# Seven block products for eight in the gate and up projections of a decoder trunk, with three chunks of inner units and the residual kept in y

## The chip, the core and the metric

The kernel runs on one core of a Trainium2 chip. The metric is device time in microseconds (us) of one execution, as the median of several. Engines are named as in the profile: PE (TensorE matmuls), PEld (its weight loads), DVE (VectorE), ACT (ScalarE), POOL (GpSimd), SP (SyncE, which here only issues DMAs).

## What is computed

A trunk of two layers over 528 tokens (16 meta tokens and 512 of the sequence), width 1024. Each layer has a feed-forward block (FFN), a mixer (a convolution branch and a recurrent branch), and a second FFN, each followed by a layer norm over the scaled input plus the block's output. The part that matters here:

```python
D_MODEL = 1024; SEQ = 512; DEPTH = 2; N_META = 16; D_FF = 2816
LN_EPS = 1e-5; ALPHA = (2 * DEPTH) ** 0.25

def _swiglu(x, wg, wu, wd):
    return (jax.nn.silu(x @ wg) * (x @ wu)) @ wd

for l in range(DEPTH):
    h = _layer_norm(ALPHA * h + 0.5 * _swiglu(h, ffn1_wg[l], ffn1_wu[l], ffn1_wd[l]), ln1_g[l], ln1_b[l])
    m = _mixer(h, ...)
    h = _layer_norm(ALPHA * h + m, ln2_g[l], ln2_b[l])
    h = _layer_norm(ALPHA * h + 0.5 * _swiglu(h, ffn2_wg[l], ffn2_wu[l], ffn2_wd[l]), ln3_g[l], ln3_b[l])
return h[:, N_META:]
```

All of it is float32. `wg` and `wu` are 1024 x 2816, `wd` is 2816 x 1024.

## The kernel before

**Data and precision.** Activations lie transposed, features on the 128 partitions and tokens along the free side: x is 8 k-tiles of 128 features by 528 tokens. Every float32 operand of a large product is split into two float32r parts, `hi` (a cast on ACT) and `lo` (the remainder, a subtraction on DVE; `split`, L101). A product of two split operands is three matmuls per k-tile: hi by hi, hi by lo, lo by hi (`mac1`, L190). The lo by lo part is left out.

**Weights.** `wunit` (L106) brings one block of up to 8 k-tiles by 128 columns (512 KB) from HBM into a `w_raw` tile (two buffers) by a DMA on SP's queue, casts it to `w_hi` on ACT (L128) and forms `w_lo` on DVE (L139). With `dma=True`, which only 32 of the mixer's blocks use, ACT writes the negated `hi` part into `w_lo` (L132) and an accumulating DMA issued by POOL adds `w_raw` to it (L133). The `w_hi`, `w_lo` pairs come from a ring of pools (`self.wring`), eight pairs in an FFN's body.

**An FFN** (`ffn`, L425). Its tokens are handled in two halves of 264 (256 in the last FFN, which leaves out the meta tokens); `tok[h]` is one half. The 2816 inner units are 22 tiles of 128, handled in two chunks of 11. In a chunk:

- `up(fc, f)`: load one gate and one up block (8 k-tiles each), and for each half multiply both with x into two PSUM banks (48 matmuls), then silu on ACT (L453), the product on DVE (L454), and the split into `hh`, `hl` (L103, L104).
- `down(fh, o)`: for one of 8 tiles of outputs, multiply `hh`, `hl` of the 11 units with two blocks of `wd`, for each half into one bank. The first chunk's result goes into `y` scaled by 0.5 (ACT, L474), and `residual` adds ALPHA times both parts of x (DVE, L420). The second chunk adds to `y` (L477) and to the running sum `ssum` (L415) of the norm.

`stream` (L151) takes the jobs in this order: load, then half 0 and half 1. The last three down jobs (`TAIL`) are run half by half: all three for half 0, then all three for half 1, so that the norm of half 0 (`layer_norm`, L364; mean and variance by matmuls with a matrix of ones, L371 and L390; square root and reciprocal, L391 and L392; then 8 tiles of x's two parts, L396, L406, L407) runs beside the products of half 1. The weights of the next stage are fetched in between (`fetch_ahead`). The first products of the next stage on half 0 (`heads(0)`, or the mixer's first three blocks) run beside the norm of half 1.

**Order.** A scheduler at build time fixes the order of each engine's instructions from the program's order, priorities and its own estimates. At run time each engine takes its instructions in that order and waits for what they need. Buffers are reused under the same waits.

PSUM has eight banks: six for products (`mm`) and two for the norms (`st`). The constants `smask` and `e1`, which only the mixer uses, lie in the constant pool.

Of the kernel before, what the change touches and what calls it, by code (L numbers as in the profile page):

```python
# [24 lines left out]
FT = F // P  # L25
FH = FT // 2
TAPS = 31
# [62 lines left out]
class Trunk:  # L90
# [10 lines left out]
    def split(self, x, hi, lo):  # L101

        return (self.nc.scalar.copy(hi, x),  # L103
                self.nc.vector.tensor_tensor(lo, x, hi.bitcast(F32), op=ALU.subtract))  # L104

    def wunit(self, *srcs, dst=None, dma=False):  # L106

        srcs = [s if isinstance(s, tuple) else (slice(0, P), s) for s in srcs]
        kt = srcs[0][1].shape[1]
        raw = self.wp.tile([P, KT, P], F32, name="w_raw", bufs=WB[0])  # L110
        if dst is None:
            pool, bufs = self.wring[self.wi % len(self.wring)]
            self.wi += 1
            dst = [pool.tile([P, KT, P], F32R, name=x, bufs=bufs) for x in ("w_hi", "w_lo")]
        hi, lo = dst
        for r, src in srcs:
            load = self.nc.sync.dma_start(out=raw[r, :kt], in_=src)
            if self.behind is not None:
                self.nosync(load, self.behind)
                self.behind = None  # L120
        n = kt // self.cuts
        for i in range(0, kt, n):
            k = slice(i, i + n)
            if self.cuts == 1 or not CUTA:
                continue
            self.nc.scalar.copy(hi[:, k], raw[:, k])
        if self.cuts == 1 or not CUTA:
            copy = self.nc.scalar.copy(hi[:, :kt], raw[:, :kt])  # L128
            if self.first is not None:
                self.nosync(copy, self.first[0])  # L130
        if dma:
            self.nc.scalar.activation(lo[:, :kt], raw[:, :kt], AF.Copy, scale=-1.0)  # L132
            self.nc.gpsimd.dma_start(out=lo[:, :kt].bitcast(F32), in_=raw[:, :kt], accum_op=ALU.add)  # L133
            return hi, lo
        if not CUTD:
            n = kt
        for i in range(0, kt, n):
            k = slice(i, i + n)
            sub = self.nc.vector.tensor_tensor(lo[:, k], raw[:, k], hi[:, k].bitcast(F32),  # L139
                                               op=ALU.subtract)  # L140
# [48 lines left out]

    def mac1(self, pm, w, x, s, nk, xk=0, first=True, last=True):  # L190

        hi, lo = w
        xh, xl = x
        for k in range(nk):
            for j, (a, b) in enumerate(((hi, xh), (hi, xl), (lo, xh))):
                self.nc.tensor.matmul(pm, a[:, k, :], b[:, xk + k, s],  # L196
                                      start=first and k == 0 and j == 0,
                                      stop=last and k == nk - 1 and j == 2)
            yield
# [23 lines left out]
    def setup(self):  # L223
# [29 lines left out]
        for h in range(2):  # L253
            for i in range(4):
# [3 lines left out]
                                        channel_multiplier=1)  # L258
        self.smask = cp.tile([P, T], F32, name="smask")
        nc.vector.memset(self.smask, 1.0)  # L260
        nc.vector.memset(self.smask[:, 0:1], 0.0)
        nc.vector.memset(self.smask[:, NM::C], 0.0)
        self.eps = cp.tile([P, 1], F32, name="eps")
        nc.vector.memset(self.eps, LN_EPS)
        self.e1 = [cp.tile([P, T + 1], F32, name=f"e1_{i}") for i in range(2)]
        for e in self.e1:
            nc.vector.memset(e[:, 0:1], 0.0)
        self.e1i = 0
        self.xh = cp.tile([P, KT, T], F32R, name="xh")
# [93 lines left out]

    def layer_norm(self, h, y, ssum, t0, n, gname, bname, pool, st, dst, vec, silu=False):  # L364

# [7 lines left out]
        for g in range(2):  # L373
# [5 lines left out]
            sqs.append(sq)  # L379
        rstd = pool.tile([P, 264], F32, name="ln_rstd", bufs=2)  # L380
        if SQ:

            nc.scalar.activation(rstd[:, 0:1], self.eps, AF.Sqrt)
        for sq in sqs:
# [26 lines left out]
    def add_sum(self, ssum, y, o, s):  # L411
        if o == 1:
            return self.nc.vector.tensor_tensor(ssum[:, s], y[:, 0, s], y[:, 1, s], op=ALU.add)
        elif o > 1:
            return self.nc.vector.tensor_tensor(ssum[:, s], ssum[:, s], y[:, o, s], op=ALU.add)  # L415

    def residual(self, y, o, s):

        for part in self.x:
            self.nc.vector.scalar_tensor_tensor(  # L420
                y[:, o, s], part[:, o, s].bitcast(F32), ALPHA, y[:, o, s],
                op0=ALU.mult, op1=ALU.add)


    def ffn(self, l, which, t0, n, gname, bname, pre, final=False, head=None, extra=()):  # L425
# [15 lines left out]
        def up(fc, f):  # L441
# [9 lines left out]
            def evac(h, ps):  # L451
                g = fp.tile([P, 264], F32, name="g", bufs=3)[:, :n]
                nc.scalar.activation(g, ps[0][:, :n], AF.Silu)  # L453
# [4 lines left out]

        def down(fh, o):
            cs = slice(o * P, (o + 1) * P)  # L460
            cuts = (0, 6), (6, FH)

            def load():
                return [self.wunit(wd[:, fh * FH + a:fh * FH + b, cs]) for a, b in cuts]

            def mac(w, h):
                pd = mm()
                return pd, [self.mac1(pd[:, :n], wi, (hh, hl), tok[h], b - a, a, a == 0, b == FH)
                            for wi, (a, b) in zip(w, cuts)]

            def evac(h, pd):
                yv = y[:, o, tok[h]]
                if fh == 0:
                    nc.scalar.mul(yv, pd[:, :n], 0.5)  # L474
                    self.residual(y, o, tok[h])
                else:
                    nc.vector.scalar_tensor_tensor(yv, pd[:, :n], 0.5, yv,  # L477
                                                   op0=ALU.mult, op1=ALU.add)
# [12 lines left out]
        def room():  # L491
# [3 lines left out]
            ssum = fp.tile([P, T], F32, name="ssum")  # L495
            hh, hl = (fp.tile([P, FH, T], F32R, name=x) for x in ("hh", "hl"))
            return y, ssum, lambda: fp.tile([P, 4, 264], F32, name="ln_sq", bufs=2).rearrange(
# [76 lines left out]
    def store(self, y, t0, n, pool, mm):  # L574
        nc = self.nc
        for i in range(SEQ // P):
            a = t0 + i * P
            ot = pool.tile([P, D], F32, name="ot", bufs=2)
            for g in range(2):
# [8 lines left out]
    def mixer(self, l, last, pre, more):  # L588
# [26 lines left out]
        self.ring(self.w0)  # L615
        mpool, self.mp = self.enter(f"mix{l}")
        self.places()
        cpool, self.cvp = self.enter(f"conv{l}")
# [915 lines left out]
```

## Time and profile before

| | |
|---|---|
| three runs | 3175.49, 3195.22 and 3193.57 us, median 3193.57 us |
| the profiled execution | span 3187.1 us from its first to its last instruction; its own time with what lies around the span is not given beside it |
| PE | 3086.5 us busy, 97%, 27172 matmuls |
| DVE | 1870.3 us, 59% |
| ACT | 1227.7 us, 39% |
| POOL | 52.4 us, 2% |
| DMA | 343.25 MB, mean 108 GB/s; queue of SP 34.1% of the 16 engines' span, queue of POOL 3.3% |
| mean granted TensorE clock | 0.976 |

In the lists of groups, a row is line, engine, operation, output <- inputs, shapes and count, then busy us, mean ns of one, then the engine's idle time just before these instructions and what ended it. A row of the windows gives a stretch (us from the span's start), its length, then the busy us and counts on PE, PEld, DVE, ACT and POOL, the granted clock (1.00 is full speed), the DMA engines' busy share and the GB/s moved. Matmuls overlap in the pipeline: the mean of one is longer than the distance from one to the next. Timeline rows are start, duration, engine, line, what; in square brackets the idle time before and what ended it.

### The profile page before, as it was taken

What the parts mean: (1) busy time and instruction counts of PE and PEld (TensorE: products, weight loads), DVE (VectorE), ACT (ScalarE), POOL (GpSimd) and SP (SyncE); (2) the same over time, 40 slices, a digit from 0 to 9 for tenths busy, and PEclk for the clock granted to TensorE, in tenths of its full rate; (3) what the DMA queues carried; (4) which work ended last, traced back from release to release, by engine and by line L of the source; (5) the groups of instructions that cost most, each with busy time, mean ns of one, the idle gap of its engine ahead of it and who ended that gap; (6) DMA issues with size and microseconds to landing.
All of it is one profiled execution on the core that took longest, in us unless ns stands there. A gap on an engine that the chain in (4) does not pass through costs nothing.

```text
span 3187.1 us, 64710 instructions
## 1 busy us (share of the span) xinstructions
PE 3086.5 (97%) x27172; PEld 2956.2 (93%) x27172; DVE 1870.3 (59%) x3811; ACT 1227.7 (39%) x2223; POOL 52.4 (2%) x132
## 2 busy tenths in 40 slices
PE   9999999999999899999999999999999999999998
PEld 8999989888888899999989999898888889999997
DVE  4343377888775766343363433778887758653435
ACT  4232154344454544232142321543454445242322
POOL 0000000000000000000000000000000000000000
PEclk9999999999998899999999999999998999999998
DMA  5232234334354552232232322343353555332321
GB/s 151 73 108 84 82 121 152 94 94 121 102 138 119 168 153 79 74 107 85 82 93 73 107 85 82 115 154 99 97 132 92 141 135 177 112 108 82 111 73 54
DMA packets 576434, 343.25 MB, mean 108 GB/s; under 512 B 87501, under 2 KB 539457, under 8 KB 576143
## 3 DMA queue, kind: packets, MB, share of 16 engines
q1 hardware_dynamic: 565422, 308.49, 34.1%
q0 software_dynamic: 6112, 22.10, 3.3%
q10 hardware_dynamic: 4608, 8.52, 0.7%
q8 instruction: 213, 3.49, 0.5%
q14 instruction: 79, 0.64, 0.1%
HBM read 270.81 MB, written 47.12 MB: 100 GB/s over the span
## 4 chain that ended last, share of the span: by engine, by line
PE 83%; DVE 6%; ACT 4%; DMA 4%; issue 2%; SPq 1%; ACTq 0%; DVEq 0%; POOLq 0%
PE mm L196 53%; PE mm L214 16%; PE sc L1127 2%; PE sc L1046 1%; PE ch L1221 1%; PE tr L1196 1%; DVE w_lo L139 1%; PE tr L1204 1%; PE ch L1213 1%; PE sc L799 1%; SPq L1095 1%; DMA a<-ascr 1%; ACT w_hi L128 1%; PE sc L931 1%; PE tr L1191 1%
## 5 line engine op out<-in xcount | busy, mean ns | idle before, releaser
L196 PE MATMUL mm<-xh,w_hi 128*128 128x264 f32 (+1 forms) x2880 | 818.6, 285 | 17.4 <-ACT xh L406 16.0
L196 PE MATMUL mm<-xh,w_lo 128*128 128x264 f32 (+1 forms) x2880 | 819.8, 285 | 0.5 <-DVE w_lo L139 0.5
L196 PE MATMUL mm<-xl,w_hi 128*128 128x264 f32 (+1 forms) x2880 | 818.1, 284 | 0.3 <-DVE xl L407 0.2
L139 DVE TENSOR_TENSOR w_lo<-w_raw,w_hi 128x1024 fp32r<-128x1024 f32 (+2 forms) x456 | 485.1, 1064 | 432.7 <-ACT w_hi L128 420.1
L128 ACT CAST w_hi<-w_raw 128x1024 fp32r<-128x1024 f32 (+2 forms) x400 | 385.3, 964 | 763.4 <-PE mm L196 524.6
L196 PEld LDWEIGHTS mm<-xh,w_hi 128*128 128x128 f32 x2880 | 544.7, 190 | 21.1 <-ACT xh L406 18.2
L196 PEld LDWEIGHTS mm<-xh,w_lo 128*128 128x128 f32 x2880 | 546.2, 190 | 0.8 <-DVE w_lo L139 0.8
L196 PEld LDWEIGHTS mm<-xl,w_hi 128*128 128x128 f32 x2880 | 545.5, 189 | 1.4 <-DVE xl L407 1.2
L196 PE MATMUL mm<-hl,w_hi 128*128 128x264 f32 (+1 forms) x1408 | 400.5, 284 | 0.0
L196 PE MATMUL mm<-hh,w_hi 128*128 128x264 f32 (+1 forms) x1408 | 400.4, 284 | 0.0
L196 PE MATMUL mm<-hh,w_lo 128*128 128x264 f32 (+1 forms) x1408 | 398.7, 283 | 0.0
L214 PE MATMUL mm<-xh,w_hi 128*128 128x264 f32 x1760 | 392.3, 299 | 6.4 <-DVE kp L749 2.9
L214 PE MATMUL mm<-xh,w_lo 128*128 128x264 f32 x1760 | 391.1, 298 | 5.8 <-DMA w_lo<-w_raw 5.7
L214 PE MATMUL mm<-xl,w_hi 128*128 128x264 f32 x1760 | 391.6, 298 | 0.0
L875 DVE SCALAR_TENSOR_TENSOR cacc<-cu,cw,cacc 128x528 f32<-128x528 f32 (+1 forms) x480 | 355.6, 752 | 3.4
L214 PEld LDWEIGHTS mm<-xh,w_hi 128*128 128x128 f32 x1760 | 286.0, 194 | 14.6 <-DVE kp L749 3.2
L214 PEld LDWEIGHTS mm<-xh,w_lo 128*128 128x128 f32 x1760 | 285.0, 194 | 13.5 <-DMA w_lo<-w_raw 6.6
L214 PEld LDWEIGHTS mm<-xl,w_hi 128*128 128x128 f32 x1760 | 285.5, 194 | 7.6 <-issue 0.4
L454 DVE TENSOR_TENSOR g<-g,mm 128x264 f32<-128x264 f32 (+1 forms) x176 | 74.6, 427 | 328.6 <-PE mm L196 317.7
L196 PEld LDWEIGHTS mm<-hh,w_lo 128*128 128x128 f32 x1408 | 265.1, 188 | 0.1
L196 PEld LDWEIGHTS mm<-hl,w_hi 128*128 128x128 f32 x1408 | 265.0, 188 | 0.2
L196 PEld LDWEIGHTS mm<-hh,w_hi 128*128 128x128 f32 x1408 | 264.5, 188 | 0.1
(312 smaller groups left out, 4323.0 us busy)
## 6 DMA issues: line engine op xcount, KB each, us to landing
w_raw<-in_w_in_dram SPq DMA_DIRECT2D x116, 512.0 KB
w_raw<-in_ffn_wg_dram SPq DMA_DIRECT2D x88, 512.0 KB
w_raw<-in_ffn_wu_dram SPq DMA_DIRECT2D x88, 512.0 KB
w_raw<-in_ffn_wd_dram SPq DMA_DIRECT2D x64, 384.0 KB
w_raw<-in_ffn_wd_dram SPq DMA_DIRECT2D x64, 320.0 KB
w_lo<-w_raw POOLq DMA_DIRECT2D x32, 512.0 KB, 5.0
w_raw<-in_rwkv_wo_dram SPq DMA_DIRECT2D x16, 512.0 KB
w_raw<-in_conv_wo_dram SPq DMA_DIRECT2D x16, 512.0 KB
```

What stands on the lines that cost most here:

```text
L128: copy = self.nc.scalar.copy(hi[:, :kt], raw[:, :kt])
L139: sub = self.nc.vector.tensor_tensor(lo[:, k], raw[:, k], hi[:, k].bitcast(F32), op=ALU.subtract)
L196: self.nc.tensor.matmul(pm, a[:, k, :], b[:, xk + k, s], start=first and k == 0 and j == 0, stop=last and k == nk - 1 and j == 2)
L214: m = nc.tensor.matmul(pm[:, h, :n], a[:, wk + k, :], b[:, xk + k, s:s + n], start=first and k == 0 and j == 0, stop=last and k == nk - 1 ...
L454: nc.vector.tensor_tensor(g, g, ps[1][:, :n], op=ALU.mult)
L799: nc.tensor.matmul(pm, w[a][r, o, :], x[b][r, s], start=j == 0, stop=j == 2)
L875: tap = nc.vector.scalar_tensor_tensor(y, x, w, y, op0=ALU.mult, op1=ALU.add)
L931: nc.tensor.matmul(tr[:, 32 * j:32 * j + 32], sq[:, k0:k0 + P], self.bones[:, ::4], start=True, stop=True)
L1046: pairs.append(nc.tensor.matmul(ps[:, e, p * P:(p + 1) * P], FB[p][r, fs], G[r, p, 1, :, cs], start=True, stop=True))
L1095: nc.sync.dma_start(out=dd[o:o + NM, g * N // 2:(g + 1) * N // 2, f, r], in_=self.xd[q, g, f, k:k + N // 2] .rearrange("s t i -> t s i"))
L1127: nc.tensor.matmul(ps[r, i, cs], vt[r, i], x[r, i, cs], start=True, stop=True)
L1191: nc.tensor.transpose(tr[0:C, p * P:(p + 1) * P], Q["v"][p][:, cs], self.ident)
```

## The change

**The scheme.** For an inner tile take x's two halves of features (k-tiles 0 to 3 and 4 to 7) and two halves of tokens as a 2 x 2 block matrix, and gate and up with their two halves of features as another. The four results (gate and up of both token halves) are eight block products. Strassen's scheme, in the form used here, gets them from seven: with sums of weight blocks (`s1` to `s4`) and sums of x blocks (`t1` to `t4`). Each block product has 4 k-tiles and 3 matmuls each: 12 matmuls into a PSUM bank.

**A seven-unit** (`up7`) loads a gate and an up block, forms the four sums on DVE, splits five pieces (`halve`): the gate block whole, `s1` and the lower block of up by ACT and an accumulating DMA each; `s2` with `s3` (whole) and `s4` by ACT and DVE. It uses four ring entries and four PSUM banks; three banks are written by a second product after the first was read. The results are joined by DVE additions from PSUM, silu on ACT, the product and the split into `hh`, `hl`.

**Where.** The first four units of each FFN (`PLAIN`) stay as they were. Beside them `make_seven` adds the two parts of x into `y` in full precision, forms `t2`, `t3`, `t4`, and at the end overwrites one block of `xh`, `xl` with `t1`. Units 4 to 21 are seven-units.

**Chunks and residual.** The inner tiles are taken in three chunks of 8, 8 and 6; a down job has one weight block. `y` already holds x, so the first chunk's down job computes 2 ALPHA y plus the product in one DVE instruction, the others add; y is twice what it was, and `layer_norm` takes 4 LN_EPS (`twice`).

**Room.** `hh` and `hl` hold 8 tiles instead of 11; `smask` and `e1` move into the mixer's pool and are set by POOL there; the evacuated gate values lie in `ln_sq` tiles, the output rows in `w_raw` tiles.

```diff
-FH = FT // 2
+CHUNKS = ((0, 8), (8, 16), (16, FT))
+PLAIN = 4
+KH = KT // 2
...
+    def halve(self, x, hi, lo, dma):
+
+        self.nc.scalar.copy(hi, x)
+        if dma:
+            self.nc.scalar.activation(lo, x, AF.Copy, scale=-1.0)
+            self.nc.gpsimd.dma_start(out=lo.bitcast(F32), in_=x, accum_op=ALU.add)
+        else:
+            self.nc.vector.tensor_tensor(lo, x, hi.bitcast(F32), op=ALU.subtract)
...
+        def up7(fc, f):
+            cs = slice(fc * P, (fc + 1) * P)
+
+            def load():
+                pool = (self.wp, fp)[fc % 2]
+                raw = [pool.tile([P, KT, P], F32, name="w_raw", bufs=2) for _ in range(2)]
+                for r, w in zip(raw, (wg, wu)):
+                    nc.sync.dma_start(out=r, in_=w[:, :, cs])
+                g1, g2, u1, u2 = (r[:, k:k + KH] for r in raw for k in (0, KH))
+                sums = fp.tile([P, 3 * KH, P], F32, name="sums", bufs=1)
+                s1 = fp.tile([P, KH, P], F32, name="sum1", bufs=2)
+                s2, s3, s4 = (sums[:, i * KH:(i + 1) * KH] for i in range(3))
+                for o, a, b in ((s1, u1, u2), (s3, g1, u1), (s2, s1, g1), (s4, s2, g2)):
+                    nc.vector.tensor_tensor(o, a, b, op=ALU.add)
+                his, los = zip(*(self.entry() for _ in range(4)))
...
+                parts = ((0, whole, raw[0], True), (2, lower, s1, True), (2, upper, u2, True),
+                         (1, whole, sums[:, :KT], False), (3, lower, s4, False))
+                for e, k, src, dma in parts:
+                    self.halve(src, his[e][:, k], los[e][:, k], dma)
+                block = lambda e, k: (his[e][:, k], los[e][:, k])
+                return [block(0, lower), block(1, lower), block(1, upper), block(2, lower),
+                        block(0, upper), block(2, upper), block(3, lower)]
+
+            def mac(w, h):
+                if h:
+                    return None, [()]
+                w1, w6, w7, w5, w2, q4, w3 = w
+                x11, x21, x22, t1, t2, t3, t4 = seven
+                run = lambda ps, w, x, first, last: self.together([
+                    self.mac1(ps[:, :n], w, x[:2], x[2], KH, x[3], first, last, True)])
+                a, b, c, d = (mm() for _ in range(4))
+                z = fp.tile([P, 4, 264], F32, name="ln_sq", bufs=2)
+                e0, e1, e2, e3 = (z[:, i, :n] for i in range(4))
+                add = lambda o, x, y: nc.vector.tensor_tensor(o, x, y[:, :n], op=ALU.add)
+                run(a, w1, x11, True, True)
+                nc.scalar.copy(e0, a[:, :n])
+                run(b, w6, t2, True, True)
+                add(e0, e0, b)
+                run(c, w7, t3, True, True)
+                add(e1, e0, c)
+                run(d, w5, t1, True, True)
+                add(e1, e1, d)
+                run(a, w2, x21, False, True)
+                nc.scalar.activation(e3, a[:, :n], AF.Silu)
+                run(c, q4, t4, False, True)
+                add(e2, e0, c)
+                out = [(hh[:, f, t], hl[:, f, t]) for t in tok]
+                close = lambda u, g, h: (nc.vector.scalar_tensor_tensor(
+                    u, u, -1.0, g, op0=ALU.mult, op1=ALU.mult), self.split(u, *out[h]))
+                close(e2, e3, 0)
+                run(d, w3, x22, False, True)
+                add(e0, e0, d)
+                nc.scalar.activation(e0, e0, AF.Silu)
+                close(e1, e0, 1)
+                return None, [()]
...
+        def make_seven():
...
+            for h in range(2):
+                for k in (0, KH):
+                    a, b = half(h, k)
+                    nc.vector.tensor_tensor(y[:, k:k + KH, tok[h]], a.bitcast(F32),
+                                            b.bitcast(F32), op=ALU.add)
+            b11, b12, b21, b22 = (y[:, k:k + KH, tok[h]] for k in (0, KH) for h in range(2))
+            p, q = (fp.tile([P, 4, 264], F32, name="ln_sq", bufs=2)[:, :, :n] for _ in range(2))
+            t2, t3, t4 = (tile(x) for x in ("t2", "t3", "t4"))
...
+            sub(q, b22, b12)
+            self.split(q, *t3)
+            sub(p, b11, b12)
+            neg(q, p, b22)
+            self.split(q, *t2)
+            neg(q, q, b21)
+            self.split(q, *t4)
+            t1 = half(1, 0)
+            yield
+            self.split(p, *t1)
...
             def load():
-                return [self.wunit(wd[:, fh * FH + a:fh * FH + b, cs]) for a, b in cuts]
+                return self.wunit(wd[:, a:b, cs])
...
             def evac(h, pd):
                 yv = y[:, o, tok[h]]
-                if fh == 0:
-                    nc.scalar.mul(yv, pd[:, :n], 0.5)
-                    self.residual(y, o, tok[h])
+                if a == 0:
+                    nc.vector.scalar_tensor_tensor(yv, yv, 2 * ALPHA, pd[:, :n],
+                                                   op0=ALU.mult, op1=ALU.add)
                 else:
-                    nc.vector.scalar_tensor_tensor(yv, pd[:, :n], 0.5, yv,
-                                                   op0=ALU.mult, op1=ALU.add)
+                    nc.vector.tensor_tensor(yv, yv, pd[:, :n], op=ALU.add)
+                if b == FT:
                     self.add_sum(ssum, y, o, tok[h])
...
-        jobs = []
-        for fh in range(2):
-            jobs += [up(fh * FH + f, f) for f in range(FH)]
-            jobs += [down(fh, o) for o in range(KT)]
+        jobs, held, seven = [], {}, []
+        for a, b in CHUNKS:
+            jobs += [(up if f < PLAIN else up7)(f, f - a) for f in range(a, b)]
+            jobs += [down(a, b, o) for o in range(KT)]
+        sums = make_seven()
+        for i in (PLAIN, PLAIN - 1):
+            jobs.insert(i, (lambda: next(sums), lambda w, h: (None, [()]), lambda h, ps: None))
...
+        self.smask = self.mp.tile([P, T], F32, name="smask")
+        nc.gpsimd.memset(self.smask, 1.0)
+        nc.gpsimd.memset(self.smask[:, 0:1], 0.0)
+        nc.gpsimd.memset(self.smask[:, NM::C], 0.0)
```

More of the change, by code (lines that the diff above doesn't have):

```diff
@@ L104, in split, with entry @@
                 self.nc.vector.tensor_tensor(lo, x, hi.bitcast(F32), op=ALU.subtract))
+    def entry(self):
+        pool, bufs = self.wring[self.wi % len(self.wring)]
+        self.wi += 1
+        return [pool.tile([P, KT, P], F32R, name=x, bufs=bufs) for x in ("w_hi", "w_lo")]
+    def halve(self, x, hi, lo, dma):
[5 more added lines that the diff above has]
+            self.nc.vector.tensor_tensor(lo, x, hi.bitcast(F32), op=ALU.subtract)
     def wunit(self, *srcs, dst=None, dma=False):
@@ L111, in wunit @@
         if dst is None:
-            pool, bufs = self.wring[self.wi % len(self.wring)]
-            self.wi += 1
-            dst = [pool.tile([P, KT, P], F32R, name=x, bufs=bufs) for x in ("w_hi", "w_lo")]
+            dst = self.entry()
         hi, lo = dst
@@ L188, in leave, with mac1 @@
         pool.__exit__(None, None, None)
-    def mac1(self, pm, w, x, s, nk, xk=0, first=True, last=True):
+    def mac1(self, pm, w, x, s, nk, xk=0, first=True, last=True, parts=False):
         hi, lo = w
@@ L197, in mac1 @@
                                       start=first and k == 0 and j == 0,
-                                      stop=last and k == nk - 1 and j == 2)
+                                      stop=last and k == nk - 1 and j == 2,
+                                      skip_group_check=parts)
             yield
@@ L258, in setup @@
                                         channel_multiplier=1)
[L259 to L268, printed above, removed]
+        self.eps = cp.tile([P, 2], F32, name="eps")
+        for i, m in enumerate((1, 4)):
+            nc.vector.memset(self.eps[:, i:i + 1], m * LN_EPS)
         self.xh = cp.tile([P, KT, T], F32R, name="xh")
@@ L361, in rsqrt, with layer_norm @@
         return y
-    def layer_norm(self, h, y, ssum, t0, n, gname, bname, pool, st, dst, vec, silu=False):
+    def layer_norm(self, h, y, ssum, t0, n, gname, bname, pool, st, dst, vec, silu=False,
+                   twice=False):
         nc = self.nc
@@ L451, in evac @@
             def evac(h, ps):
-                g = fp.tile([P, 264], F32, name="g", bufs=3)[:, :n]
+                if h == 0:
+                    held[fc] = fp.tile([P, 4, 264], F32, name="ln_sq", bufs=2)
+                g = held[fc][:, h, :n]
                 nc.scalar.activation(g, ps[0][:, :n], AF.Silu)
@@ L457, in up @@
             return load, mac, evac
-        def down(fh, o):
+        def up7(fc, f):
[12 more added lines that the diff above has]
+                his, los = zip(*(self.entry() for _ in range(4)))
+                lower = slice(0, KH)
+                upper = slice(KH, KT)
+                whole = slice(0, KT)
+                parts = ((0, whole, raw[0], True), (2, lower, s1, True), (2, upper, u2, True),
[37 more added lines that the diff above has]
+                return None, [()]
+            return load, mac, lambda h, ps: None
@@ L577, in store @@
             a = t0 + i * P
-            ot = pool.tile([P, D], F32, name="ot", bufs=2)
+            ot = pool.tile([P, KT, P], F32, name="w_raw", bufs=2).rearrange("p k c -> p (k c)")
             for g in range(2):
@@ L616, in mixer @@
         mpool, self.mp = self.enter(f"mix{l}")
+        self.smask = self.mp.tile([P, T], F32, name="smask")
+        nc.gpsimd.memset(self.smask, 1.0)
+        nc.gpsimd.memset(self.smask[:, 0:1], 0.0)
+        nc.gpsimd.memset(self.smask[:, NM::C], 0.0)
+        self.e1 = [self.mp.tile([P, T + 1], F32, name=f"e1_{i}") for i in range(2)]
+        for e in self.e1:
+            nc.gpsimd.memset(e[:, 0:1], 0.0)
+        self.e1i = 0
         self.places()
```

32 lines of the change are left out of this document (20 added, 12 removed).

## The prediction

> **What bounds the kernel now.** I read the page from the top: busy times first, then the chain that ended last, then the windows of the feed-forward (FFN) bodies, then the ends of the FFNs.
>
> ```profile
> PE 3086.5 (97%) x27172; PEld 2956.2 (93%) x27172; DVE 1870.3 (59%) x3811; ACT 1227.7 (39%) x2223; POOL 52.4 (2%) x132
> PE mm L196 53%; PE mm L214 16%; PE sc L1127 2%; PE sc L1046 1%; PE ch L1221 1%; PE tr L1196 1%; DVE w_lo L139 1%; PE tr L1204 1%; PE ch L1213 1%; PE sc L799 1%; SPq L1095 1%; DMA a<-ascr 1%; ACT w_hi L128 1%; PE sc L931 1%; PE tr L1191 1%
> ```
>
> PE is busy in 97% of the span, and L196, the product helper of the FFNs, carries 53% of the chain. A busy PE could still be a PE that waits for weights, so the windows inside the FFNs come next (columns: length, busy time and count on PE, PEld, DVE, ACT, POOL, granted clock, DMA share, GB/s).
>
> ```profile
> 1235.00:1592.00 357.00, 356.94 (x2934) 356.91 (x2934) 138.53 (x218) 107.59 (x182) 0.00 (x0) 1.00 0.33 95
> 2804.00:3150.00 346.00, 345.85 (x2924) 345.65 (x2924) 134.08 (x214) 104.94 (x181) 0.00 (x0) 1.00 0.32 92
> ```
>
> Inside an FFN PE never stops, at clock 1.00, while DVE is at 39%, ACT at 30% and the DMA engines at 33%. So a matmul removed there is time removed, as long as the helpers keep up. One matmul costs 357/2934 = 0.1217 us with 264 columns and 346/2924 = 0.1183 us with 256 (the last FFN). A plain unit (gate and up, 8 k-tiles, 3 split products, 2 halves: 96 matmuls) takes 11.7 us.
>
> **The change part by part.** *Matmuls.* A seven-product unit has 7 x 4 x 3 = 84 matmuls: 12 fewer. 18 of the 22 units of each of 4 FFNs change, so 864 matmuls go; those of the down products stay 1056 per FFN. 648 x 0.1217 + 216 x 0.1183 = 104.4 us. A seven-unit takes 84 x 0.1217 = 10.2 us of PE, and everything that feeds it must fit in that.
>
> *Feeding a seven-unit.* The prices:
>
> ```profile
> L139 DVE TENSOR_TENSOR w_lo<-w_raw,w_hi 128x1024 fp32r<-128x1024 f32 x272 | 332.7, 1223 | 275.2 <-ACT w_hi L128 272.4 <-PE mm L328 0.9
> L128 ACT CAST w_hi<-w_raw 128x1024 fp32r<-128x1024 f32 x272 | 285.2, 1049 | 486.9 <-PE mm L196 257.9 <-PE mm L214 83.8 <-DMA w_raw<-in_ffn_wu_dram 43.3
> L126 ACT CAST w_hi<-w_raw 128x512 fp32r<-128x512 f32 x120 | 72.4, 616 | 92.7 <-PE mm L214 52.0 <-issue 27.6 <-DMA w_raw<-in_w_in_dram 10.1
> L454 DVE TENSOR_TENSOR g<-g,mm 128x264 f32<-128x264 f32 x132 | 56.3, 429 | 253.1 <-PE mm L196 245.2 <-ACT g L453 7.0 <-PE mm L319 0.8
> L103 ACT CAST hh<-g 128x264 fp32r<-128x264 f32 x132 | 53.9, 413 | 172.8 <-DVE g L454 172.8
> L139 DVE TENSOR_TENSOR w_lo<-w_raw,w_hi 128x512 fp32r<-128x512 f32 x56 | 38.2, 682 | 5.7 <-ACT w_hi L126 4.9 <-ACT w L1198 0.4
> L132 ACT ACTIVATE w_lo<-w_raw 128x1024 fp32r<-128x1024 f32 x32 | 33.8, 1056 | 0.2
> L133 POOL DMA_DIRECT2D w_lo<-w_raw x32 | 27.7, 866 | 441.3 <-ACT w_lo L132 131.6 <-PE sc L1037 63.9 <-PE sc L1046 61.4
> ```
>
> DVE: four sums of 512 columns (4 x 0.682), two low parts (1.223 + 0.682) and nine operations of 264 columns to join the products (9 x 0.43): 8.5 us. ACT: high parts of 1024 twice and 512 three times (2 x 1.049 + 3 x 0.616), three negations (1.056 + 2 x 0.616) and five evacuations (5 x 0.41): 8.3 us. Before, a plain unit took 2 x 1.223 + 4 x 0.43 = 4.2 us of DVE and 2 x 1.049 + 4 x 0.41 = 3.7 us of ACT. Both engines double and still fit in 10.2 us, with 2 us to spare. DMA is nearer the edge: 1 MB of weights as before, and now three accumulating DMAs (1 MB) that POOL issues.
>
> ```profile
> 1340.00:1440.00 100.00, 100.00 (x822) 100.00 (x822) 41.88 (x67) 30.10 (x50) 0.00 (x0) 1.00 0.36 104
> 2589.00:2592.00 3.00, 3.00 (x48) 2.76 (x46) 2.90 (x14) 0.00 (x0) 0.00 (x0) 1.00 0.92 175
> DMA to landing us min/median/max: 4.5/5.0/7.1
> ```
>
> Weights move at 104/0.36 = 289 GB/s of engine time, 3.6 us per MB. The second row is one accumulation of 512 KB alone: 175/0.92 = 190 GB/s, so 5.5 us per MB. Together 9.1 us of 10.2: the fullest resource after PE. The third row is the time from issue to landing of the accumulations of w_lo. The Trainium skill ("DMA: Bandwidth & Descriptors", Anatomy of one DMA) gives a DMA from GpSimd as about 2.0 us plus bytes over 436 GB/s, which for 512 KB would be an estimate of 3.2 us; the 5.0 us of the trace speak against it for an accumulation. By its price the accumulations would fill only 2.4 us of a unit, no stall would be left, and the sum below would be 22 us lower.
>
> Do the transfers come in time? Eight weight buffers, four to a unit, let one unit be prepared while another runs. A raw slot serves every second unit, so its chain must fit in 2 x 10.2 = 20.4 us.
>
> ```profile
> 1244.06 0.37 SPq L117 DMA_DIRECT2D w_raw<-in_ffn_wg_dram  x1
> 1246.40 0.37 SPq L117 DMA_DIRECT2D w_raw<-in_ffn_wu_dram  x1
> 1250.30 1.05 ACT L128 CAST w_hi<-w_raw 128x1024 fp32r<-128x1024 f32 x1 [1.17 <-DMA w_raw<-in_ffn_wu_dram]
> L214 PE MATMUL mm<-xh,w_lo 128*128 128x264 f32 x1760 | 391.1, 298 | 5.8 <-DMA w_lo<-w_raw 5.7
> ```
>
> Both loads: 6.2 us from first issue to use (1244.06 to 1250.30). High parts and negations of the three parts that go by DMA: 2.1 + 4 x 0.62 = 4.6. POOL's issue 0.9, landing 5.0, and the two half accumulations behind the first 1.4 more: 18.1 us. It fits, with 2 us of slack. What waits at times: in the mixer, 32 such accumulations held PE up for 5.7 us, 0.18 us each, with two buffers in the ring. The FFNs will have 216 of them (3 x 72), with eight buffers but a fuller DMA. No row shows this mixture; the ends are 0 and the price of the second rival. I take 0.1 us each, near the mixer's row: 22 us. A wait also holds back what is queued behind it: a cast waiting for a load stands in front of ACT's copy of the first product, which DVE's joins and the reopened bank of the fifth product wait for (3 products, 4.4 us of cover); the banks that DVE must read before the sixth and seventh have 2.9 us.
>
> *Setting up the sums of x.* Four adds, four differences and four low parts of 1056 columns (1.25 us each, between the 1024-row and its 3% more) are 15 us of DVE per FFN, in the first four plain units, 47 us in which DVE is free for 61%. Only the last (the rewrite of x's own lower block, which must wait for the fourth unit's last matmul) comes late: 1.1 us on ACT and 1.25 on DVE, needed by the fourth product of the next unit, 4.4 us later. Ends 0 and the 15; I take 1 us per FFN, 4 us. If the cover goes, that wait is the first to show.
>
> *The end of an FFN.* The last three down jobs run half by half, and the second halves cover the first norm. They had 3 x 33 matmuls, now 3 x 18 (the last chunk has 6 units): 45 x 0.1217 = 5.5 us less cover.
>
> ```profile
> 395.00:437.00 42.00, 34.39 (x255) 32.79 (x253) 32.27 (x58) 17.59 (x28) 2.68 (x7) 0.92 0.10 26
> 1575.00:1627.00 52.00, 44.82 (x338) 43.44 (x337) 37.13 (x60) 19.37 (x26) 0.00 (x0) 0.93 0.31 90
> 1990.00:2032.00 42.00, 35.23 (x250) 33.57 (x249) 31.40 (x56) 16.57 (x26) 1.90 (x4) 0.88 0.11 30
> 3150.00:3187.00 37.00, 22.54 (x145) 18.82 (x143) 24.88 (x42) 15.22 (x27) 0.00 (x0) 0.77 0.14 57
> PE mm L196 <- ACT xh L406: 5.3, 1, 5.3
> 1600.49 1.05 ACT L128 CAST w_hi<-w_raw 128x1024 fp32r<-128x1024 f32 x1 [2.69 <-PE mm L196]
> ```
>
> At the two FFN-to-mixer ends PE already idles 7 us while DVE is busy 32 of 42: the norm sets the pace, so lost cover is lost time, 2 x 5.5. Between the FFNs (1575) the 5.3 us wait came after a cast that waited for a weight buffer still in use by the tail; the tail's six buffers become three, so I take +1 there (ends -5.3 and +5.5). At the very end norm and store already run largely alone: +3 (ends 0 and 5.5). Sum +15.
>
> *The rest.* The residual into y turns one ACT and two DVE operations per output into one DVE operation, off the path: 0. Masks written by POOL at each mixer's start: under 1 us of POOL beside PE's heads, 1 us in all (ends 0 and 4).
>
> **Sum.** -104.4 + 22 + 4 + 15 + 1 = -62. The profiled execution spans 3187.1 us; its own whole time is not shown, the three runs have 3175.49 to 3195.22, and the median 3193.57 is 6.5 above the span. 3193.6 - 62 = 3131 us.
>
> **The rivals.** *One wait per unit in a fixed order.* The cast above stood 1.17 us at the head of ACT's queue for its load; before, nothing urgent stood behind it. If one such wait per seven-unit reaches PE, 72 x 1.17 = 84 us take the place of the 22: 3193 us, no change. For it: loads now share the engines with accumulations. Against: 2.9 us of cover.
>
> *Slower: the raw slot's chain.* If the sums (2.7 us of DVE) and the neighbour's five evacuations (2.0 on ACT) stand inside it, POOL issues three times in it (2.6) and landing takes the 7.1 of the worst row, it is 6.2 + 2.7 + 4.6 + 2.0 + 2.6 + 7.1 = 25.2 us, 12.6 per unit against 10.2. From 20.4 us on it costs; from about 23.7 on it eats the gain. The first two units of each chunk are prepared under the down products, so 48 units pay 2.4 us: +115, 3222 us. Stalls may also slow the clock:
>
> ```profile
> 1606.35 1.22 PE L371 MATMUL st<-ssum,ones 128*128 128x264 f32 x2 [1.92 <-DVE ssum L415]
> 1604.00:1608.00 4.00, 2.08 (x9) 1.70 (x8) 4.00 (x9) 2.47 (x3) 0.00 (x0) 0.79 0.44 129
> 1608.00:1612.00 4.00, 4.00 (x29) 4.00 (x28) 3.64 (x10) 3.03 (x8) 0.00 (x0) 0.78 0.00 0
> ```
>
> After 1.9 us of idling the clock was 0.79 and 0.78 over 8 us, a loss of 1.7 us; on all 48 units 82 us more. So 3222 to 3304, and 3245 if one stall in four goes cold. The Trainium skill ("TensorE: Matmul & The Clock Gate", What you observe and What's actually happening) halves the clock only after an idle window of some 3.4 us; here a gap of 1.9 us was followed by a slow stretch, so the row decides, and by the rule this rival would stay at 3222.
>
> *Better: no stalls, and lost cover only at the two mixers.* -104.4 + 11: 3100 us.
>
> **How the numbers follow.** A measurement of this kernel tells about 1% from no change: 3162 to 3225. Forecast 0.46 (3131, its own range 3108 to 3165), one wait per unit 0.22 (3193), slower chain 0.20 (3245), better 0.12 (3100). The range 3095 to 3240 leaves out the far half of the slower case and a sliver below the better one. Faster: 0.12 + 0.46 less 0.03 for the edge of the forecast, 0.55; same 0.25; slower 0.20.
>
> **What will show it.** 26308 PE instructions; a seven-unit near 10.2 us of unbroken PE at clock 1.00 and DMA share near 0.9 there (the forecast); waits of PE or of its weight loads for w_lo or for the joins, over 1 us in most units (the first rival) or over 2 with clock under 0.9 (the second); PE idle at 395 and 1990's counterparts up from 7 to some 12 us. Wrong outright would be my count of DMA time, if short accumulating rows move slower than the long ones seen here.

## The result: no faster, where 62 us less were forecast

The changed kernel takes 3209.99 us (median) against 3192.12 for the kernel before on the same chip: a ratio of 1.0059, 95% interval 1.0033 to 1.0085, so half a per cent slower. The prediction was 3131 us. The profiled execution spans 3208.3 us (before 3187.1). One of the changed kernel's seven executions took 5013 us at a granted clock of 0.72; the ratio leaves it out.

From the page of the changed kernel, the busy times, the queue of the accumulating DMAs, and the chain that ended last:

```profile
PE 3022.6 (94%) x26308; PEld 2878.5 (90%) x26308; DVE 2177.7 (68%) x4471; ACT 1496.6 (47%) x2649; POOL 239.4 (7%) x358
...
q0 software_dynamic: 37216, 97.62, 17.3%
...
PE 65%; DMA 12%; DVE 9%; issue 9%; ACT 4%; POOL 1%; SPq 0%; ACTq 0%; POOLq 0%; DVEq 0%
PE mm L210 34%; PE mm L229 17%; DMA w_raw<-in_ffn_wu_dram 4%; DMA w_raw<-in_ffn_wd_dram 3%; DMA w_lo<-w_raw 3%; DVE w_lo L153 2%; PE sc L1236 2%; ACT w_hi L142 1%; PE sc L1155 1%; PE tr L1305 1%; PE ch L1330 1%; PE tr L1313 1%; PE ch L1322 1%; POOL w_lo L118 1%; DMA a<-ascr 1%
```

The 864 matmuls are gone (27172 to 26308) and PE is busy 64 us less. But it is now busy for 94% of the span, not 97%; the product helper's share of the chain fell from 53% to 34%, and loads and accumulations stand in it. The time went into gaps. Windows of the changed kernel show them (length, busy time and count on PE, PEld, DVE, ACT, POOL, granted clock, DMA share, GB/s): the second FFN, a gap in it and the 8 us behind that, and a stretch of the first FFN.

```profile
1260.00:1590.00 330.00, 313.24 (x2498) 309.56 (x2497) 194.11 (x348) 164.63 (x272) 46.42 (x54) 0.98 0.66 150
1420.00:1424.00 4.00, 1.30 (x11) 1.08 (x10) 1.19 (x4) 2.88 (x6) 1.34 (x3) 0.89 0.99 223
1424.00:1428.00 4.00, 4.00 (x18) 4.00 (x19) 2.66 (x6) 0.97 (x3) 0.50 (x1) 0.50 1.04 181
1428.00:1432.00 4.00, 4.00 (x28) 4.00 (x27) 2.62 (x6) 1.07 (x3) 0.00 (x0) 0.75 0.73 216
60.00:80.00 20.00, 2.82 (x16) 2.79 (x17) 7.97 (x13) 3.98 (x6) 0.86 (x1) 0.50 0.38 90
```

PE idles 17 us in 330 at clock 0.98, where it never stopped at 1.00 before. After a gap of 2.70 us it got through 18 and 28 matmuls in 4 us each, at clock 0.50 and 0.75, where 33 fit at full speed. So the gap cost its 2.7 us and some 2.4 again. In the first FFN PE stood still for most of 20 us. The waits say for what (engine and line, what ended the wait, us in total, times, longest):

```profile
SPq L470 <- DMA w_lo<-w_raw: 780.4, 110, 32.8
DVE sum L476 <- DMA w_raw<-in_ffn_wu_dram: 164.8, 53, 7.9
PE mm L210 <- DVE ln_sq L499: 33.0, 20, 2.9
PE mm L336 <- DMA ln_sq<-in_conv_w_dram: 22.8, 1, 22.8
PE mm L210 <- ACT ln_sq L457: 5.9, 2, 3.0
PE mm L210 <- DVE t2l L106: 4.8, 2, 2.5
```

Read from the top, the first three are one story. SP holds a seven-unit's loads (L470) until the accumulation that read the raw slot has landed. DVE then stands 53 times, 3.1 us on average, at the sum s1 (L476), which waits for its up block. And PE stands 20 times for a join (L499); ten of these waits, 22.6 of the 33.0 us, come right behind an s1 that stood for its load. One instance, from the timeline (start, length, engine, line):

```profile
1412.03 0.86 POOL L118 DMA_DIRECT2D w_lo<-w_raw  x1 [0.33 <-issue]
...
1417.89 0.37 SPq L470 DMA_DIRECT2D w_raw<-in_ffn_wu_dram  x1
...
1419.35 0.68 DVE L476 TENSOR_TENSOR sums<-sums,w_raw 128x512 f32<-128x512 f32 x1
1422.84 0.69 DVE L476 TENSOR_TENSOR sum<-w_raw 128x512 f32<-128x512 f32 x1 [2.81 <-DMA w_raw<-in_ffn_wu_dram]
1423.45 0.42 DVE L499 TENSOR_TENSOR ln_sq<-ln_sq,mm 128x264 f32<-128x264 f32 x1
...
1423.93 0.59 PE L210 MATMUL mm<-xh,w_hi 128*128 128x264 f32 x1 [2.70 <-DVE ln_sq L499]
```

The accumulation issued at 1412.03 frees the up block's slot; the load goes out at 1417.89 and is there at 1422.84. Until then DVE has nothing to do, since s1 heads its queue. The join that frees the bank PE needs comes after it, and PE starts at 1423.93. Yet nothing reads s1 before the other sums of its unit (the s1 before this one ran at 1412.87 and was first read at 1418.41). Those have a single buffer and come once that is free; s1 has two buffers, so the build-time order could put it this early.

The last row is the same story at the first seven-unit of an FFN: in the second FFN DVE ran an s1 at 1282.28 after standing 5.06 us for its load, the low part of t2 came right behind it, and PE could use that at 1284.19.

The fourth row is another matter: the transposes of `conv_w` (`layer_vectors`, an `extra` job of the first FFN) wait for a load into an `ln_sq` buffer.

### The profile page after: what moved, and what is told of

It reads as the page before. It is cut to its first block, busy times and chain, and to the rows that moved or that the text cites. A ratio compares the mean times of both kernels' runs of the same rounds, so it can differ in the third digit from the quotient of the medians.

```text
span 3208.3 us, 64745 instructions
## 1 busy us (share of the span) xinstructions
PE 3022.6 (94%) x26308; PEld 2878.5 (90%) x26308; DVE 2177.7 (68%) x4471; ACT 1496.6 (47%) x2649; POOL 239.4 (7%) x358
## 4 chain that ended last, share of the span: by engine, by line
PE 65%; DMA 12%; DVE 9%; issue 9%; ACT 4%; POOL 1%; SPq 0%; ACTq 0%; POOLq 0%; DVEq 0%
PE mm L210 34%; PE mm L229 17%; DMA w_raw<-in_ffn_wu_dram 4%; DMA w_raw<-in_ffn_wd_dram 3%; DMA w_lo<-w_raw 3%; DVE w_lo L153 2%; PE sc L1236 2%; ACT w_hi L142 1%; PE sc L1155 1%; PE tr L1305 1%; PE ch L1330 1%; PE tr L1313 1%; PE ch L1322 1%; POOL w_lo L118 1%; DMA a<-ascr 1%
## 5 line engine op out<-in xcount | busy, mean ns | idle before, releaser
L210 PE MATMUL mm<-xh,w_hi 128*128 128x264 f32 (+1 forms) x1728 | 501.7, 291 | 48.8 <-DVE ln_sq L499 22.6
L210 PE MATMUL mm<-xl,w_hi 128*128 128x264 f32 (+1 forms) x1728 | 499.9, 290 | 0.4
L210 PE MATMUL mm<-xh,w_lo 128*128 128x264 f32 (+1 forms) x1728 | 498.4, 289 | 0.0
L142 ACT CAST w_hi<-w_raw 128x1024 fp32r<-128x1024 f32 (+1 forms) x224 | 227.8, 1018 | 430.7 <-PE mm L210 157.6
L153 DVE TENSOR_TENSOR w_lo<-w_raw,w_hi 128x1024 fp32r<-128x1024 f32 (+2 forms) x280 | 303.5, 1084 | 157.6 <-ACT w_hi L142 151.0
L210 PEld LDWEIGHTS mm<-xh,w_hi 128*128 128x128 f32 x1728 | 334.1, 194 | 55.7 <-DVE ln_sq L499 25.1
L210 PEld LDWEIGHTS mm<-xl,w_hi 128*128 128x128 f32 x1728 | 335.7, 194 | 1.8 <-DVE xl L417 1.6
L210 PEld LDWEIGHTS mm<-xh,w_lo 128*128 128x128 f32 x1728 | 335.6, 194 | 0.1
L229 PEld LDWEIGHTS mm<-xh,w_hi 128*128 128x128 f32 x1760 | 287.4, 195 | 16.0 <-DVE kp L858 3.2
L229 PEld LDWEIGHTS mm<-xh,w_lo 128*128 128x128 f32 x1760 | 286.4, 195 | 12.3 <-DMA w_lo<-w_raw 4.1
L229 PEld LDWEIGHTS mm<-xl,w_hi 128*128 128x128 f32 x1760 | 286.5, 194 | 7.6 <-issue 0.2
L118 POOL DMA_DIRECT2D w_lo<-w_raw x144 | 124.3, 864 | 1319.9 <-ACT w_lo L117 658.4
```

The source lines that it names most:

```text
L118: self.nc.gpsimd.dma_start(out=lo.bitcast(F32), in_=x, accum_op=ALU.add)
L210: self.nc.tensor.matmul(pm, a[:, k, :], b[:, xk + k, s], start=first and k == 0 and j == 0, stop=last and k == nk - 1 and j == 2, skip_gro ...
L229: m = nc.tensor.matmul(pm[:, h, :n], a[:, wk + k, :], b[:, xk + k, s:s + n], start=first and k == 0 and j == 0, stop=last and k == nk - 1 ...
```

## Experiments

The theories, by the letters that the expectations use. **Q**: the order in DVE's queue, s1 at its head, is the cause. **S**: the raw slots come free late, because accumulations that read them land late, and late loads cost whatever the order. **B**: the DMA engines are simply full. **V**: the `conv_w` load waits for buffers that `p` and `q` of `make_seven` hold. Ratios are to the kernel before, run on the same chip; a difference of ratios is turned into time with the 3186 us of before.

| kernel | us | ratio (95%) |
|---|---|---|
| changed kernel | 3209.99 | 1.0059 (1.0033 to 1.0085) |
| e1 vectors earlier | 3213.41 | 1.0099 (1.0061 to 1.0136) |
| e2 s1 tied | 3140.2 | 0.9875 (0.9855 to 0.9896) |
| e3 accumulations from the sums | 3282.67 | 1.0327 (1.0309 to 1.0344) |
| e4 no accumulations | 3132.12 | 0.985 (0.9821 to 0.988) |
| e5 vectors among the down jobs | 3193.28 | 1.0025 (1.0002 to 1.0048) |
| e6 = e2 + e5 | 3127.57 | 0.9821 (0.979 to 0.9851) |
| e7 = e2 + e5 + e4 | 3116.94 | 0.9785 (0.9758 to 0.9811) |
| e8 = e2 + e5, one accumulation | 3105.77 | 0.9751 (0.9725 to 0.9776) |
| e9 = e5, one accumulation | 3116.48 | 0.9781 (0.975 to 0.9811) |
| e10 = e8, three plain units | 3136.01 | 0.9838 (0.9806 to 0.9869) |
| e11 = e8, chunks 6, 8, 8 | 3106.08 | 0.9753 (0.9725 to 0.9781) |
| e12 = e5 + e4 | 3111.26 | 0.9771 (0.9742 to 0.9799) |

**s1 tied behind s3 (e2).**

```diff
-for o, a, b in ((s1, u1, u2), (s3, g1, u1), (s2, s1, g1), (s4, s2, g2)):
-    nc.vector.tensor_tensor(o, a, b, op=ALU.add)
+add = lambda o, a, b: nc.vector.tensor_tensor(o, a, b, op=ALU.add)
+third = add(s3, g1, u1)
+self.nosync(add(s1, u1, u2), third)
+add(s2, s1, g1)
+add(s4, s2, g2)
```

> The sum s3 (gate block and up block) comes first, and s1 (of two up blocks) is tied behind it on DVE, so that no sum that waits for its load stands at the head of DVE's queue some microseconds ahead of its use, with the joins of the unit before behind it. Theory Q (DVE's order is the cause: joins late, banks late, PE idles and then runs cold): PE's waits for joins (8 us per FFN) and the clock after them come back, 30 to 60 us: 3150 to 3180. Theory S (the raw slots come free late, because the accumulations that read them land late; loads are then late whatever DVE's order): within 8 us of 3210. Theory B (the DMA engines are simply full): the same as S.

Measured: 3140.2 us, 59 us (of ratio) under the changed kernel, with the same instructions. Its waits:

```profile
SPq L470 <- DMA w_lo<-w_raw: 758.6, 109, 32.1
DVE sums L475 <- DMA w_raw<-in_ffn_wu_dram: 22.4, 15, 3.2
PE mm L210 <- DVE ln_sq L502: 5.8, 6, 1.5
```

And a window of its second FFN:

```profile
1260.00:1560.00 300.00, 297.67 (x2424) 295.38 (x2423) 187.32 (x338) 154.29 (x258) 43.75 (x51) 1.00 0.71 161
```

SP waits for the accumulations as often and as long as in the changed kernel, so the loads still go out when they did. But DVE no longer stands there (164.8 to 22.4 us), the joins come in time (33.0 to 5.8 us of PE), and PE runs almost through at clock 1.00. Q holds; S and B, by which the order would not matter, fall. In the profiled executions the stretches that hold the inner units of the four FFNs are 60 us shorter (25 to 391, 1252 to 1976 and 2824 to 3149 us of the changed kernel against 25 to 377, 1239 to 1931 and 2765 to 3076 here): PE idles 43 us less, 27 of them waits for joins and 10 the rows of L457 and t2l, and it is busy 17 us less with as many matmuls, an estimate of the clock's share.

**Which reads are accumulated (e3).**

```diff
-parts = ((0, whole, raw[0], True), (2, lower, s1, True), (2, upper, u2, True),
-         (1, whole, sums[:, :KT], False), (3, lower, s4, False))
+parts = ((0, whole, raw[0], False), (2, upper, u2, False), (2, lower, s1, True),
+         (1, whole, sums[:, :KT], True), (3, lower, s4, True))
```

> The same number of low-part columns by DVE (1536) and by accumulating DMA (2048) as in the changed kernel, but other ones: what is read from the raw slots goes by DVE, what is read from the sums and s1 by DMA. A raw slot is then free as soon as the two engines have read it, some 7 us sooner. Theory S (raw slots held until accumulations land): loads come in time, the waits of the sums for their loads (53 per kernel, 165 us of DVE idling) shrink to under a third, 3210 becomes 3150 to 3180. Theory B (DMA engines full): within 8 us of 3210, or slower, since the one buffer of sums is now held by an accumulation (up to 40 us slower). Theory Q: within 15 us of 3210.

Measured: 3282.67 us, slower than any theory had it. The waits of this kernel:

```profile
DVE sums L476 <- DMA w_lo<-sums: 107.2, 54, 7.5
DVE sum L476 <- DMA w_lo<-sum: 88.2, 25, 4.8
DVE sum L476 <- DMA w_raw<-in_ffn_wu_dram: 65.3, 26, 7.6
PE mm L210 <- DVE ln_sq L499: 60.4, 40, 4.7
```

With the same bytes in accumulations DVE waits less for the up blocks (164.8 to 65.3 us), as the first half of S has it, though not under the third that S named; and some of the fall may come from DVE standing elsewhere. For the sums now wait for the accumulations that read their own buffers, 195 us at the head of the same queue, and PE's waits for joins nearly double. Here too what heads DVE's queue holds PE up, though it waits for something else.

**No accumulations (e4).** All five parts of `load` have `False`.

> No accumulating DMAs in the feed-forward products: all low parts by DVE, which gets 2048 more columns per seven-unit (2.5 us) and comes to some 11 us in 10.2 of PE. Theory B (DMA engines full) and theory S (slots held by accumulations): DMA share falls from 0.95 to about 0.4, the waits for loads go, and what is left is DVE as the bound, 0.5 to 0.8 us for each of some 60 units: 3150 to 3185. Theory Q (order in DVE's queue, whatever the DMAs do): the joins still wait in that queue and DVE is fuller: 3220 to 3270.

Measured: 3132.12 us, better than S and B expected and against Q as I had worded it there. A window of its second FFN:

```profile
1260.00:1560.00 300.00, 295.81 (x2407) 294.59 (x2407) 223.42 (x388) 124.78 (x207) 0.00 (x0) 0.99 0.34 98
```

In this window of the second FFN the DMA share is 0.34. DVE, at 223 of 300, is no bound. DVE still stands 21 times at s1, 53.9 us, but PE waits only 1.2 us for joins. So the early s1 costs little when its load is seldom late: the loss needs both, late loads and the order.

**The vectors (e1, e5).** e1 puts the two `layer_vectors` jobs at places 2 and 3 of the job list (`4 + 4 * l` to `2 + l`), e5 among the first chunk's down jobs (`12 + 3 * l`).

> The two jobs that load the layers' vectors come two places earlier (both ahead of the third plain unit), so that the 31-row load of conv_w takes its ln_sq buffer before the differences p and q do. Theory V (conv_w's load waits for a buffer that p and q hold; PE then idles 22.8 us and runs cold after it): the wait of the transposes L336 goes, the first FFN gets some 25 us shorter, 3210 becomes 3183 to 3188. Rival (the start of the kernel waits for the loads of x and of the first weights anyway, and the wait only moves): 3205 to 3212.

> The changed kernel with one edit: the two jobs that load the layers' vectors stand among the down jobs of the first chunk, where nothing takes an ln_sq buffer. Theory V2 (the wait of the conv_w transposes, 22.8 us of PE idle in the first FFN and the cold clock behind it, comes from p, q and the plain units holding the ln_sq buffers at that place; two places earlier only moved it): first FFN some 25 us shorter, 3210 becomes 3180 to 3188. Rival (whatever the place, PE's queue holds the transposes ahead of products while SP is still loading vectors): 3203 to 3212.

In the changed kernel, three rows of the timeline:

```profile
68.49 1.26 DVE L106 TENSOR_TENSOR t4l<-ln_sq,t4h 128x1056 fp32r<-128x1056 f32 x1 [1.14 <-ACT t4h L105]
...
69.78 0.25 SPq L324 DMA_DIRECT2D ln_sq<-in_conv_w_dram  x1
...
77.18 1.03 PE L336 MATMUL mm<-ident,ln_sq 31*128 31x31 f32 x8 [22.77 <-DMA ln_sq<-in_conv_w_dram]
```

The load goes out 0.03 us after the last read of `q`, whose buffer it takes, and PE has the transposes at the head of its queue since 54. In e1 the wait broke into three, and nothing was won (1.0099 against 1.0059, intervals overlapping):

```profile
50.40 1.06 PE L336 MATMUL mm<-ident,ln_sq 31*128 31x31 f32 x8 [8.41 <-DMA ln_sq<-in_conv_w_dram]
57.33 0.45 PE L327 MATMUL mm<-ident,ssum 128*128 128x128 f32 x1 [5.86 <-DMA ssum<-in_time_mix_dram]
64.42 1.03 PE L336 MATMUL mm<-ident,ln_sq 31*128 31x31 f32 x8 [6.42 <-DMA ln_sq<-in_conv_w_dram]
```

There the buffer was free, and the transposes still stood ahead of products while their loads were on the way. In e5 they have no wait left, and the stretch from 60 to 80 us, for which PE was busy 2.82 us, reads:

```profile
60.00:80.00 20.00, 16.93 (x127) 16.71 (x126) 14.49 (x20) 10.08 (x16) 1.71 (x2) 0.91 0.34 81
```

The time fell by 11 us of ratio, less than the 25 expected, and the intervals overlap. V2 is right about the place; half of the gain is missing here (3 us of PE still idle in this stretch). The same move is worth 17 us with s1 tied (e2 to e6) and 25 without accumulations (0.985 to 0.9771, e4 to e12), both with intervals apart.

**Both (e6), and with fewer accumulations (e7, e8, e9, e12).** In e8 and e9 only the gate block is accumulated (`True` on the first part alone).

> s3 first with s1 tied behind it, and the vector jobs among the down jobs. If the two losses are separate, they add: 3140 less some 22 (18.7 us of idling on conv_w were left with s1 tied, and some 4 of cold clock): 3112 to 3122. If they share a cause: within 6 us of 3140.

> As the kernel before it in this series (s1 tied, vectors among the down jobs), but all low parts by DVE. Theory Q (late loads hurt only through DVE's queue): taking away the accumulations has nothing left to give, and DVE gets fuller: within 12 us of the same kernel with accumulations. Theory S/B (the accumulations also cost by themselves, through loads that come late): another 15 to 40 us faster than it.

> s1 tied, vectors among the down jobs, and one accumulation of 512 KB per seven-unit (the gate block) in place of three: 1024 more columns for DVE, 512 KB less for the DMA engines. Between the two neighbours if the price of each side is even: within 6 us of their mean. If DVE near 10 us of a unit's 10.2 costs, slower than both by up to 15 us; if the accumulations cost, as fast as the one without any.

> One accumulation of 512 KB per seven-unit and the vectors among the down jobs, but the sums in the order of the changed kernel: s1 first, not tied. Tying s1 was worth some 66 us with three accumulations (3193 to 3128) and, after the 17 us of the vectors, nothing without any (3115 to 3117). Theory Q (an early s1 costs only as often as its load comes late, and the loads are late because accumulations hold the raw slots): between, some 10 to 35 us slower than with s1 tied (3106): 3116 to 3140. Rival (the order counts only with the two further accumulations, which hold the slot of the up block): within 6 us of 3106.

> No accumulations, the vectors among the down jobs, s1 first and not tied: the third point of a row. Tying s1 was worth 2.0% of the time before with three accumulations per unit (1.0025 to 0.982) and 0.3% with one (0.978 to 0.975). Theory Q (an early s1 costs as often as its load comes late): with none it is worth nothing that can be told, a ratio of 0.976 to 0.981 against 0.9785 with s1 tied. Rival (an early s1 costs by itself): 0.983 or more.

e6 gives 3127.57 us. e7 takes 11 us less, inside Q's 12 and short of the 15 to 40 of S and B, though with overlapping intervals. The vectors are worth 17 us on top of the tie (0.9875 to 0.9821), where 22 were expected, so the two losses are separate. The tie, always with the vectors moved: 65 us with three accumulations per unit (1.0025 to 0.9821), 10 with one (0.9781 to 0.9751), nothing with none (0.9771 to 0.9785); the last two pairs have overlapping intervals. The wait at s1 without the tie, with one accumulation (first two rows, e9) and with none (e12):

```profile
DVE sum L476 <- DMA w_raw<-in_ffn_wu_dram: 105.7, 44, 6.1
PE mm L210 <- DVE ln_sq L499: 2.7, 3, 1.8
```

```profile
DVE sum L476 <- DMA w_raw<-in_ffn_wu_dram: 55.1, 21, 5.3
```

DVE's waits fall from 164 (e5, three accumulations) to 106 and 55 us, and PE's waits for joins from 30.5 (e5) to 2.7 already with one: most waits at the head of DVE's queue no longer reach PE. e9 ended at the low end of Q's range, near the rival's (3116 where 3106 was the same kernel tied); it doesn't tell them apart. e12 answers another question: without accumulations the early s1 costs nothing that can be told.

e8 beats both kernels: 0.9751, 2.5% under before, 3.1% under the changed one. Against e6 two accumulations less are worth 22 us, the intervals just apart; against e7 they overlap. It is faster than any case that was expected of it, and why one should do better than none is not shown.

**Two more steps on e8 (e10, e11).** `PLAIN = 3`, and `CHUNKS = ((0, 6), (6, 14), (14, FT))`.

> The fastest kernel so far (s1 tied, vectors among the down jobs, one accumulation) with three plain units per feed-forward in place of four: 48 matmuls fewer, 48 x 0.121 = 5.8 us. If the set-up of the sums of x (15 us of DVE) fits under the third unit and the heads: 3098 to 3102. If it comes late by its own length in one unit of each: 3106 to 3125.

> The fastest kernel so far with chunks of 6, 8 and 8 units in place of 8, 8 and 6: the last three down jobs have 24 matmuls a half in place of 18, so the first norm has 18 matmuls, 2.2 us, more cover at each of the four ends. Theory (lost cover at the ends is lost time, as the prediction had it): 4 to 9 us faster, 3097 to 3102. Rival (the ends are set by the norm's own chain, or the shorter first chunk takes as much): within 3 us of 3106.

e10 is slower by 28 us of ratio, outside both cases expected. Its waits, of e10 first and e8 behind:

```profile
PE mm L210 <- ACT hh L105: 11.8, 11, 2.2
```

```profile
PE mm L210 <- ACT hh L105: 4.3, 3, 2.2
```

The expected wait for the sums of x isn't there; down products wait for the inner units (`hh`) 7.5 us longer, which doesn't explain 28, least of all with 6 us of matmuls saved. The cause stays open.

e11 took the same time as e8. The first norm's end and the end between the FFNs, of e8 and then of e11:

```profile
379.00:421.00 42.00, 31.84 (x219) 29.98 (x219) 32.88 (x60) 18.27 (x29) 3.17 (x12) 0.88 0.09 26
1531.00:1583.00 52.00, 43.75 (x326) 42.05 (x324) 41.81 (x74) 19.60 (x30) 0.00 (x0) 0.90 0.32 91
```

```profile
379.00:421.00 42.00, 34.07 (x228) 32.20 (x226) 32.23 (x60) 16.92 (x28) 1.80 (x4) 0.88 0.09 26
1546.00:1598.00 52.00, 47.10 (x353) 45.55 (x351) 40.17 (x70) 20.03 (x30) 0.00 (x0) 0.93 0.27 76
```

PE idles 2.2 and 3.4 us less at these ends, as the theory of lost cover says, but the whole doesn't show it; with a spread of 17 us among the runs of e11, 4 to 9 us could hide. Not settled.

## Why the prediction was wrong, step by step

- **The matmuls** were right in number: 864 fewer. PE's busy time fell by 64 us in the changed kernel, where 104.4 were counted on, but by 94 and 95 in e2 and e8, which have as many matmuls. The 30 us between the changed kernel and e2 are an estimate of what the slower clock took (mean granted clock 0.964 against 0.975).
- **"It fits, with 2 us of slack"** (the raw slot's chain). By the prediction's own 5.5 us per MB the two half accumulations are 2.8 us, not 1.4, so 1 us of slack was left, not 2. SP's waits for landings say that the chain was tight. But e2 has the same waits of SP, and there DVE waits for up blocks only 22.4 us: a tight chain alone was not what failed. In the instance above it took 5.9 us from the up block's accumulation to its slot's next load, the 0.9 and 5.0 assumed. The landings in the changed kernel:

```profile
w_lo<-w_raw POOLq DMA_DIRECT2D x104, 512.0 KB, 4.9
w_lo<-w_raw POOLq DMA_DIRECT2D x72, 256.0 KB, 5.2
```

  The median of the whole blocks (32 of the 104 are the mixers') is 4.9 us against 5.0 before, so it did not stretch; the slowest of all these landings took 8.6 us (7.1 before). In e3, where a 512 KB accumulation follows one of 256 KB, the median was 6.4.
- **"I take 0.1 us each ... 22 us"**, the stalls, is the term that was mis-sized, and the step that failed is the one on what stands behind a wait. The order of DVE's queue cost 59 to 65 us (e2 and e6). I looked for what is queued behind a wait and named ACT's cast, with its evacuation behind it. The sums are on DVE, and behind s1 stand joins of the unit that PE is working on, three of its five in the instance above; the order of sums and joins I never asked for. The first rival, one wait per unit in a fixed order, is this mechanism with 0.22 and on another engine: 1.17 us a unit there, 3.1 us each at 53 places here, of which ten held PE up directly. The wait that the rival named occurs too, but it isn't the loss: ACT's casts of down blocks wait 78.2 us for their loads in the changed kernel and 87.3 in e2.
- **The clock** stood only in the second rival, priced by one gap of 1.9 us (without the clock that rival's sum comes to 3224 us, not 3222). Here it went by the length of the gap: of the 16 gaps of PE over 1 us that a join (L499) ended, the five of 2.54 to 2.95 us left it at 0.50 to 0.60 over the next 4 us, the eleven of 1.24 to 2.18 us at 1.00. Gaps with other causes don't part there: one of 1.88 us, ended at 2815.38, left it at 0.57. The Trainium skill ("TensorE: Matmul & The Clock Gate", What's actually happening) halves the clock after an idle window of about 3.4 us; all these gaps were shorter, and six of them were followed by the drop, so the measurement decides.
- **The `ln_sq` buffers** were in no term. `p` and `q` share the two buffers with the first FFN's `conv_w` load, and the transposes of what it loads head PE's queue: 22.8 us in the profile, 11 to 25 us of time.
- **The set-up of x's sums**, 4 us: waits of PE for L457 and t2l are 10.7 us in the changed kernel, more than twice that. But they stand behind s1 as the joins do: with s1 tied (e2) 0.7 us of both is left. So the cover that I counted on was there, and this is part of what the order cost.
- **The ends**, 15 us. The counterparts of the four windows shown before:

```profile
417.00:459.00 42.00, 31.95 (x216) 30.07 (x215) 32.88 (x60) 17.74 (x28) 2.73 (x10) 0.88 0.10 26
1596.00:1648.00 52.00, 43.47 (x323) 41.99 (x322) 41.10 (x72) 18.74 (x28) 0.00 (x0) 0.90 0.33 92
2002.00:2044.00 42.00, 32.23 (x221) 30.00 (x220) 32.87 (x60) 18.27 (x29) 3.17 (x12) 0.88 0.09 26
3171.00:3208.00 37.00, 21.21 (x118) 16.51 (x116) 25.13 (x44) 15.22 (x27) 0.00 (x0) 0.68 0.14 57
```

  PE idles 10.1 and 9.8 us at the mixers (7.6 and 6.8 before), 8.5 between the FFNs (7.2) and 15.8 at the end (14.5). About half of what I took.
- **The sum without the two losses**: e6, in which both are mended and nothing of the arithmetic is changed, stands 57 us under before, and the prediction said 62. Its other terms were right together, not one by one: the ends were half of what I took, and PE's busy time fell by 88 us, not 104. That the two come so near is partly luck. What the accumulations still cost with s1 tied, 11 to 22 us (e7 and e8 against e6), is of the size of the 22 taken for stalls.

## What to carry to other kernels

When a change gives an engine new work that waits for a transfer, ask where in that engine's queue it will stand, and what of the work in hand stands behind it; a total of busy time that fits says nothing on this. An operation whose output isn't needed yet should not stand ahead of the joins that PE waits for, least of all where its input can be late; here one tie (a dependency without a semaphore, which only fixes the order) was worth 2%. And list every user of each buffer that a change borrows, one-off loads included.

## What the runs showed of the hardware

A 512 KB accumulation lands 4.9 us after its issue (median) in a kernel whose FFNs run the DMA engines at shares up to 1.04, and 5.0 in the kernel before, in the mixers; behind one of 256 KB it took 6.4 (e3). Gaps of PE of 2.5 to 3 us behind a join cost more than their length: after one of 2.70 us, 46 matmuls ran in 8 us instead of 66. Gaps of up to 2.2 us behind a join cost only themselves: after one of 2.18 us, 33 matmuls ran in the next 4 us at a clock of 1.00.
